# The last head of the second layer: V's split and Silu behind the first scores, its gates kept on chip, two output tiles loaded one head ahead

## The chip, the cores and the metric

The kernel runs on one core of one Trainium2 chip. The metric is the device time of one execution in microseconds. The engines are called as the profile calls them: PE (TensorE matmul), PEld (its weight load), DVE (VectorE), ACT (ScalarE), POOL (GpSimd) and SP (SyncE, which issues most DMAs).

## The reference

Two layers over 1024 latent tokens and 256 context tokens of width 1024. Layer 0 is multi-head latent attention, layer 1 differential attention; the change lies in layer 1, of which only the latent stream is returned.

```
q, k, v, gate = split(h @ w_in, 4)              # 8 heads of two 64-wide q/k pairs, v 128 wide; rope on q, k
for each head, m in (0, 1):                     # keys: 1024 latent and 256 context tokens
    o_m = softmax(q_m k_m^T / 8) v
o = rms_norm(o_1 - lam * o_2, g_sub) * (1 - lambda_init)
o = o * silu(gate)                              # all heads side by side: 1024 wide
x = layer_norm(alpha * x + ada_gate * (o @ out_w[1]), ln_g, ln_b)
```

## The kernel before

Values are split into a high and a low part, and a product is three matmuls (`mm3`: high x high, high x low, low x high). So nearly every operand has a pair of tiles: `vh`/`vl` for V, `ph`/`pl` for the turned probabilities, `oH`/`oL` for the output weight.

Layer 1 runs head by head (`H1` = 8), and in a head over eight query tiles of 128 rows. `step1` is one step. It issues for tile t the scores (`scores1`: PSUM banks `b`, maxima on DVE at L1360 and L1364, Exp on ACT at L1370, the combination of the two softmaxes on DVE at L1376), for tile t-2 the values (`values1`, L1391 to L1393, then `o` on ACT at L1396 and L1397), and for tile t-1 the turns of the probabilities (`turn1`, L1383) with their split into `ph` (ACT, L181) and `pl` (DVE, L182). Between these pieces it draws work from a generator `side`, by credits given in `SLOT1` or `SLOTO`. In heads 0 to 6 the side work is the projection of the next head (`prod_k1`, `prod_q1`, `prod_v1`) and the preparation of weights; the projection of V leaves V in `Vf`, the raw gates in `gg`, and a closure `top` in the list `later`, which splits V, applies the Silu and stores the gates in DRAM (`sg_d`, L1333). In head 6 the side work also holds the output weight: four slices by `out_w1`, four by `out_pre`, which loads and scales them into the buffers `z` and `res`.

In the last head (`last`, h = 7) the side work is the output projection. `out_open` runs ahead of its first step: it opens a pool for the gates (`g`, two buffers), loads the layer norm's gain, loads tiles 0 and 1 (`out_load`: the seven finished heads of `o` from `o_d`, all gates from `sg_d`, and their product on POOL at L1484) and splits the four prepared weight slices (L1473, L1474 and the helper `split` at L176 and L177). Each tile is then turned (`out_turns`, seven transposes at L1496), multiplied by the output weight (`out_tile1`, `mm3` at L185 to L187), given the eighth turn of the last head's slice, and normalised. In step t of the last head the side work is `out_tile1(t - 2)` with `out_turns(t - 1)` woven in; in step 2 `out_turns(0)` goes first; steps 0 and 1 have none.

The order on PE is the order in the program (`manual_schedule` with `MAN1 = 'P'`). On the other engines and on SP's queue a planner sets the order when the kernel is built, by program order among what its own cost model holds ready. Each engine then works its list in order. PSUM has eight banks, all under the tag `b` in this layer; a bank is bound to its next tile by the planner. Tiles of SBUF rotate by tag: `ws` has three buffers, `wsq` one, `p0` two, `p1` one, `vh` and `vl` two.

Of the kernel before, what the change touches and what calls it, by code (L numbers as in the profile page):

```python
# [9 lines left out]
F32 = mybir.dt.float32  # L10
# [3 lines left out]
AF = mybir.ActivationFunctionType  # L14
ALU = mybir.AluOpType
AX = mybir.AxisListType

P = 128
# [35 lines left out]
def hybrid_kernel(  # L54
# [40 lines left out]
    def spool(name, **kw):  # L95
        return tc.tile_pool(name=name, bufs=1, reuse_waits="tile", **kw)
# [5 lines left out]
    def rot(pool_, shape, dt, tag, bufs=1, first=False):  # L102

        if not first and (id(pool_), tag) in pre:
            return pre.pop((id(pool_), tag))
        t = pool_.tile(shape, dt, tag=tag, bufs=bufs, name=nm(tag))
        if first:
            pre[id(pool_), tag] = t
        return t
# [69 lines left out]
    def split16(hi, lo, src, scale):  # L179

        act.activation(hi, src, AF.Copy, scale=scale)  # L181
        dve.scalar_tensor_tensor(lo, src, scale, hi, op0=ALU.mult, op1=ALU.subtract)  # L182
# [384 lines left out]
    def chain(*gs):  # L567
        for g in gs:
            yield from g
# [406 lines left out]
    def w1(tag):  # L976
        sh, d, b = TAG1[tag]
        return rot(place[tag], sh, d, tag, b)
# [70 lines left out]
    with ow_ctx, spool("o0") as op0:  # L1049
# [96 lines left out]
        for t in range(8):  # L1146
# [53 lines left out]

    TAGP = {"cosB": ([P, SEQ], F32, 1), "sinB": ([P, SEQ], F32, 1), "rsw": ([P, 512], F32, 1),
            "kr": ([P, NTOK], F32, 1), "kH": ([P, NTOK], F16, 1), "kL": ([P, NTOK], F16, 1)}
    TAGV = {"rr": ([P, 512], F32, 1), "gg": ([P, SEQ // P, P], F32, 1), "Vf": ([P, NT, P], F32, 1)}

    TAGO = {"res": ([P, D], F32, 2), "z": ([P, D], F32, 2), "gb3": ([P, D], F32, 1),
            "bs": ([P, 2, 6], F32, 2), "mv": ([P, 4], F32, 2)}
# [9 lines left out]
    wo4 = a1.enter_context(spool("a1ow", side="right"))  # L1216
    oHL = [[wo4.tile([P, D], F32R, name=f"oH1{k}"), wo4.tile([P, D], F32R, name=f"oL1{k}")] for k in range(NOW)]
    gate1 = wo4.tile([P, D], F32, name="gate1")
    wv1 = prv.enter_context(spool("a1projv", side="right"))
    for k_, v_ in TAGV.items():  # L1220
        rot(wv1, v_[0], v_[1], k_, v_[2], first=True)
# [7 lines left out]
    def weave(main, side, at):  # L1229

        for i, v in enumerate(main):
            if i in at:
                next(side, None)
            yield v
        yield from side
# [67 lines left out]
    def prod_v1(h):  # L1303
        w, uv = wt[1], un[1]
        gg, Vf = w1("gg"), w1("Vf")
        vt[h] = vh, vl = w1("vh"), w1("vl")
        vT = w1("rr")[:, :CTX]
        ps = bank("b")
        for k in range(KT):
            mm3(ps[:, :CTX], w[k][0][:, :P], w[k][1][:, :P], h1H[:, k, SEQ:], h1L[:, k, SEQ:], k == 0, k == KT - 1)  # L1310
            if k % 2:
                yield 6 * CTX
        act.copy(vT, ps[:, :CTX])  # L1313
        for t in (0, 1, 2, 8, 3, 4, 9, 5, 6, 7):
            ts = slice(t * P, (t + 1) * P)
            ps = bank("b")
            if t < 8:
                for k in range(KT):
                    mm3(ps[:, :256], h1H[:, k, ts], h1L[:, k, ts], *w[k], k == 0, k == KT - 1)
                    if k % 2:  # L1320
                        yield 6 * 276
            else:
                pe.transpose(ps[:, :P], vT[:, (t - 8) * P:(t - 7) * P], idn)
                yield 256
            act.copy(Vf[:, t, :], ps[:, :P])
            if t < 8:
                act.copy(gg[:, t, :], ps[:, P:256])

        def top():
            split16(vh, vl, Vf, kc1)  # L1330
            g = gg.rearrange("p t d -> p (t d)")
            act.activation(g, g, AF.Silu, scale=uv)
            sp.dma_start(sg_d[1][:SEQ, h * P:(h + 1) * P].rearrange("(t p) d -> p t d", p=P), gg)  # L1333

        later.append(top)
        yield 0

    def scores1(h, t):
# [48 lines left out]
    def values1(h, t, ph, pl, sm):  # L1387
        vh, vl = vt[h]
        ps = bank("b")[:, :P]
        for kc in range(NT):  # L1390
            pe.matmul(ps, ph[:, kc, :], vh[:, kc, :], start=kc == 0, stop=False)  # L1391
            pe.matmul(ps, ph[:, kc, :], vl[:, kc, :], start=False, stop=False)  # L1392
            pe.matmul(ps, pl[:, kc, :], vh[:, kc, :], start=False, stop=kc == NT - 1)  # L1393
        o, o2, ss = w1("o1"), w1("o2"), w1("ss")
        pool.tensor_tensor(sm[:, 5:6], sm[:, 2:3], us1[h], op=ALU.mult)  # L1395
        act.activation(o, ps, AF.Copy, scale=sm[:, 5:6])  # L1396
        act.activation(o2, o, AF.Square, accum_out=ss[:, 0:1])  # L1397
        rstd_of(ss[:, 1:2], ss[:, 0:1], 1.0 / P, 1)
        if h == H1 - 1:
            oo, g = og[t]  # L1400
            c = slice(h * P, (h + 1) * P)
            dve.scalar_tensor_tensor(oo[:, c], o, ss[:, 1:2], g[:, c], op0=ALU.mult, op1=ALU.mult)
            return
        pool.tensor_scalar(o, o, ss[:, 1:2], None, op0=ALU.mult)
        sp.dma_start(o_d[1][t * P:(t + 1) * P, h * P:(h + 1) * P], o)
# [41 lines left out]
    def out_pre(k):  # L1447

        w = w1(("z", "res")[k % 2])
        sp.dma_start(w, out_w[1, k * P:(k + 1) * P, :])  # L1450
        yield
        if k % 2:
            act.activation(w, w, AF.Copy, scale=gsub)
        pool.tensor_tensor(w, w, gate1, op=ALU.mult)
        pre.append(w)
        yield

    def out_open():

        prv.close()  # L1460
        wg1 = a1.enter_context(spool("a1outg"))
        place["g"] = wg1
        TAG1["g"] = ([P, D], F32, 2)
        og["gb2"] = w1("wsq")
        bcast_row(og["gb2"], ln_g[1:2, :])
        rest = [big.tile([P, 5, D], F32R, tag=tg, name=nm("o1")) for tg in ("bigA", "bigB")]
        oHL.extend([r[:, k - NOW, :] for r in rest] for k in range(NOW, KT))
        out_load(0)
        for k, w in enumerate(pre):
            if k % 2:  # L1470
                split(*oHL[NOW + k], w, e_lo=pool)
            else:
                act.activation(oHL[NOW + k][0], w, AF.Copy, scale=gsub)  # L1473
                dve.scalar_tensor_tensor(oHL[NOW + k][1], w, gsub, fv(oHL[NOW + k][0]), op0=ALU.mult, op1=ALU.subtract)  # L1474
            if k == 0:
                out_load(1)

    def out_load(t):

        ts = slice(t * P, (t + 1) * P)  # L1480
        o, g = og[t] = w1("ws"), w1("g")
        sp.dma_start(o[:, :DH], o_d[1][ts, :DH])
        sp.dma_start(g, sg_d[1][ts, :])
        pool.tensor_tensor(o[:, :DH], o[:, :DH], g[:, :DH], op=ALU.mult)  # L1484

    oT = {}

    def out_turn(t, k0, n):

        o, _ = og[t]  # L1490
        if k0 == 0:
            oT[t] = [w1(tg).bitcast(F32R).rearrange("p (a b) -> p a b", a=KT) for tg in ("wx", "wy")]
        tH, tL = oT[t]
        tb = bank("b")
        for j in range(n):
            pe.transpose(tb[:, j * P:(j + 1) * P], o[:, (k0 + j) * P:(k0 + j + 1) * P], idn)  # L1496
        f = lambda x: x[:, k0:k0 + n, :].rearrange("p a b -> p (a b)")
        split(f(tH), f(tL), tb[:, :n * P])

    def out_turns(t):  # L1500
        if t >= SEQ // P:
            return
        out_turn(t, 0, 4)
        yield 1024
        out_turn(t, 4, 3)
        yield 768
# [57 lines left out]
    with tc.manual_schedule(engines={ENG[c] for c in MAN1}):  # L1564
# [38 lines left out]
        def v_last(h):  # L1603
            while later:
                later.pop(0)()
            out_early()
            yield from weave(prod_v1(h), chain(*[out_w1(k, lambda: w1("ws")) for k in range(NOW)],
                                               *[out_pre(k) for k in range(NOW, KT)]), range(1, 36, 2))

        g1 = gate_row1()  # L1610
        part = lambda h: (v for _, v in zip(range(4 if h else 0), g1))
        for h in range(H1):
            last = h == H1 - 1
            if not last:
                G = chain(weave(weave(chain(prod_k1(h + 1), prod_q1(h + 1, 0), prod_q1(h + 1, 1)), part(h), (1, 9, 17, 25)),
                                prod_w(h + 1, 1), WAT[0]),
                          weave(prod_v1(h + 1), prod_w(h + 2, 0), WAT[1]) if h + 2 < H1 else v_last(h + 1))
            else:
                while later:
                    later.pop(0)()  # L1620
                out_open()
            for t in range(SEQ // P):
                if last:
                    if t >= 2:
                        out_load(t)
                    G = weave(out_tile1(t - 2), out_turns(t - 1), (9, 12)) if t >= 2 else iter(())
                    if t == 2:
                        G = chain(out_turns(0), G)
                    credit[0] = 0
                step1((h, t), G, SLOT1 if not last else SLOTO)  # L1630
                if last:
                    for _ in G:
                        pass
            for _ in G:
                pass
        for t in range(SEQ // P - 2, SEQ // P):
# [79 lines left out]
```

## Time and profile before

| | |
|---|---|
| Time, median of 3 runs | 1776.72 us (1774.41 to 1779.07) |
| The profiled execution | 1777.68 us |
| its span, first to last instruction | 1775.8 us |
| PE busy | 1662.7 us, 94% |
| DVE busy | 1225.1 us, 69% |
| ACT busy | 1117.2 us, 63% |
| POOL busy | 822.2 us, 46% |
| mean granted clock of PE | 0.993 |

Times in the profile count from the first instruction. The last head runs from about 1615 us to the end. In a timeline a row gives start, length, engine, line, operation, the tile written and the tiles read, and in brackets how long the engine stood idle before it and what released it. A line of a helper (L176, L177, L181, L182, L185 to L187) serves many callers; the names of the tiles tell which.

### The profile page before, as it was taken

Reading aid. Unit: us, or ns where it says so; the run is one execution under the profiler, and the core shown is the slowest. Engines: PE = TensorE matmul, PEld = TensorE weight load, DVE = VectorE, ACT = ScalarE, POOL = GpSimd, SP = SyncE. Lnnn points to the kernel's source line nnn. Section 1 sums busy time; section 2 is a strip of 40 time slices with the busy share of each in tenths; the row PEclk is TensorE's granted clock in tenths of the full one; section 3 lists DMA queues with packets and bytes.
Section 4 is the critical chain, followed back from the end, with each engine's and each line's share of the span. In section 5 each row is a group of like instructions: output and inputs, shape, how many; then the busy total and the mean of one; then the engine's idle time right before and its main releaser. Section 6 shows DMA issues by size and latency. Waiting matters only on the chain. (4 is left out here: it accounts for less than half of the span.)

```text
span 1775.8 us, 36794 instructions
## 1 busy us (share of the span) xinstructions
PE 1662.7 (94%) x14564; PEld 1232.4 (69%) x14564; DVE 1225.1 (69%) x2037; ACT 1117.2 (63%) x2235; POOL 822.2 (46%) x740
## 2 busy tenths in 40 slices
PE   7999999999999999899999999999999999988998
PEld 7999966556666565577867666767676757666876
DVE  7658675566665667646855778787877777878664
ACT  2551177677777777845635676767677766758542
POOL 1432147667777676846552323231414132455454
PEclk9999999999999999999999999999999999999999
DMA  8258520110111112155532213131312122241332
GB/s 302 85 151 258 165 69 22 41 45 21 42 46 28 37 55 69 57 176 187 166 101 61 78 54 80 55 81 55 79 43 69 41 57 62 66 127 67 109 111 71
DMA packets 111225, 154.84 MB, mean 87 GB/s; under 512 B 13415, under 2 KB 84679, under 8 KB 111054
## 3 DMA queue, kind: packets, MB, share of 16 engines
q1 hardware_dynamic: 102654, 144.90, 27.5%
q10 hardware_dynamic: 8400, 7.61, 1.3%
q8 instruction: 114, 1.87, 0.4%
q14 instruction: 57, 0.47, 0.1%
HBM read 98.65 MB, written 27.07 MB: 71 GB/s over the span
## 5 line engine op out<-in xcount | busy, mean ns | idle before, releaser
L779 POOL TENSOR_TENSOR pl<-p,ph 128x1024 f16<-128x1024 f32 (+1 forms) x176 | 365.4, 2082 | 150.0 <-ACT ph L778 123.4
L1370 ACT ACTIVATE p<-ps_b,mx 128x512 f32<-128x512 f32 (+1 forms) x384 | 230.2, 616 | 65.6 <-DVE mx L1366 64.6
L777 ACT ACTIVATE p<-ps_a,esc 128x1024 f32<-128x1024 f32 (+1 forms) x176 | 189.0, 1074 | 97.4 <-PE ps_a L835 91.3
L759 DVE TENSOR_REDUCE mx<-ps_a 128x1 f32<-128x1024 f32 x128 | 155.2, 1222 | 131.2 <-PE ps_a L757 131.1
L778 ACT CAST ph<-p 128x1024 f16<-128x1024 f32 (+1 forms) x176 | 177.1, 1006 | 5.5
L1364 DVE TENSOR_REDUCE mx<-ps_b 128x1 f32<-128x512 f32 x256 | 165.4, 680 | 0.4 <-PE ps_b L1348 0.3
L848 PE MATMUL ps_d<-Vh,pl 128*128 128x65 f16 x1344 | 146.6, 194 | 3.1 <-POOL pl L779 3.1
L845 PE MATMUL ps_d<-Vh,ph 128*128 128x65 f16 x1344 | 148.7, 195 | 0.0
L847 PE MATMUL ps_d<-Vl,ph 128*128 128x64 f16 x1344 | 147.5, 193 | 0.0
L845 PEld LDWEIGHTS <-ph 128*128 128x128 f16 x1344 | 123.7, 98 | 18.3 <-issue 5.2
L1347 PE MATMUL ps_b<-KS,QS 128*128 128x512 f16 (+1 forms) x384 | 126.5, 347 | 7.7 <-DVE pl L182 4.5
L847 PEld LDWEIGHTS <-ph 128*128 128x128 f16 x1344 | 124.3, 99 | 12.3 <-issue 0.5
L1395 POOL TENSOR_TENSOR sm<-sm,us 128x1 f32<-128x1 f32 x64 | 18.5, 288 | 245.9 <-DVE sm L1374 241.9
L833 PE MATMUL ps_a<-qH,KH 100*128 100x512 f16 x320 | 122.6, 383 | 9.1 <-ACT p L777 4.3
L1348 PE MATMUL ps_b<-KS,Q 128*128 128x512 f16 (+1 forms) x384 | 129.7, 347 | 0.0
L1383 PE MATMUL ps_b<-idr,p 128*128 128x128 f32 x640 | 102.7, 276 | 28.3 <-ACT rr L1313 7.8
L182 DVE SCALAR_TENSOR_TENSOR pl<-ps_b,lcf,ph 128x512 f16<-128x512 f32 (+1 forms) x192 | 116.8, 653 | 14.3 <-ACT ph L181 14.3
L848 PEld LDWEIGHTS <-pl 128*128 128x128 f16 x1344 | 123.5, 98 | 4.3 <-POOL pl L779 4.2
L181 ACT ACTIVATE ph<-ps_b,lcf 128x512 f16<-128x512 f32 (+1 forms) x192 | 115.4, 649 | 13.2 <-PE ps_b L1383 13.2
L834 PE MATMUL ps_a<-qH,KL 96*128 96x512 f16 x320 | 122.5, 383 | 0.0
L835 PE MATMUL ps_a<-qL,KH 96*128 96x512 f16 x320 | 121.9, 381 | 0.0
L1383 PEld LDWEIGHTS ps_b<-idr,p 128*128 128x128 f32 x640 | 77.0, 141 | 54.2 <-ACT p L1370 10.9
(438 smaller groups left out, 5293.6 us busy)
## 6 DMA issues: line engine op xcount, KB each, us to landing
ws<-in_dw SPq DMA_DIRECT2D x28, 512.0 KB, 4.1
adw<-in_ada_w SPq DMA_DIRECT2D x24, 512.0 KB, 4.7
adaw<-in_ada_w SPq DMA_DIRECT2D x16, 512.0 KB, 7.9
g<-sg_d SPq DMA_DIRECT2D x16, 512.0 KB, 9.1
sg_d<-gg ACTq DMA_DIRECT2D x40, 128.0 KB, 3.6
o_d<-op SPq DMA_DIRECT2D x7, 640.0 KB, 3.8
xt<-in_xT SPq DMA_DIRECT2D x16, 256.0 KB, 4.4
wgs<-in_w_in SPq DMA_DIRECT2D x32, 128.0 KB, 3.2
```

Source lines behind the costliest of these rows:

```text
L759: dve.tensor_reduce(mx[:, t, 0:1], ps, axis=AX.X, op=ALU.max)
L777: act.activation(p32[:, :n], st, AF.Exp, scale=esc0)
L778: act.copy(ph[:, :n], p32[:, :n])
L779: pool.tensor_tensor(pl[:, :n], p32[:, :n], ph[:, :n], op=ALU.subtract)
L845: pe.matmul(pv[:, t, :], ph[:, ts], Vh[:, k, h, :], start=(k == kcs[0] and t == 0), stop=False, skip_group_check=True)
L847: pe.matmul(pv[:, t, :V0], ph[:, ts], Vl[:, k, h, :], start=False, stop=False, skip_group_check=True)
L848: pe.matmul(pv[:, t, :], pl[:, ts], Vh[:, k, h, :], start=False, stop=(k == NT - 1), skip_group_check=True)
L1347: pe.matmul(out, qs[m][:, ts], ks[m][:, c0:c0 + n], start=True, stop=False)
L1348: pe.matmul(out, q1[m][:, ts], ks[m][:, c0:c0 + n], start=False, stop=True)
L1364: dve.tensor_reduce(mx[:, 2 + 2 * m + i:3 + 2 * m + i], b, axis=AX.X, op=ALU.max, negate=True)
L1370: act.activation(p[m][:, c0:c0 + n], b, AF.Exp, bias=nb, accum_out=sm[:, 2 + 3 * m + i:3 + 3 * m + i])
L1383: pe.transpose(st[:, j * P:(j + 1) * P], pc[:, (k0 + j) * P:(k0 + j + 1) * P], idn)
```

## The change

`prod_v1` of the last head no longer puts `top` in `later`: it leaves `Vf`, `gg` and the gates' scale in the dictionary `og`. A new function `out_gates` runs behind step 1 of the last head. It takes a new pair `vh`/`vl`, splits V, closes the pool of `Vf`, opens a pool in its place with one tile `g7`, and writes the Silu of the gates there. The last head's gates are not stored to DRAM; L1402, which applies them to the last head's slice, reads `g7`.

`gg` moves to a pool that stays open. Tiles 2 to 7 load their seven eighths of the gates into it, so the pool `a1outg` with two buffers `g` goes. Tiles 0 and 1 are loaded in head 6, by `out_first` in the chain of `v_last`, with their gates in `wsq`: tile 0 between `out_w1` and `out_pre`, tile 1 behind `out_pre`. The gain `gb2`, which also lives in `wsq`, comes behind them.

The split of the four weight slices moves from `out_open` to the generator `out_split`, the side work of step 0, and `out_turns(0)` becomes the side work of step 1.

```
     def prod_v1(h):
...
-        later.append(top)
+        if h < H1 - 1:
+            later.append(top)
+        else:
+            og.update(Vf=Vf, gg=gg, uv=uv)
...
         if h == H1 - 1:
-            oo, g = og[t]
-            c = slice(h * P, (h + 1) * P)
-            dve.scalar_tensor_tensor(oo[:, c], o, ss[:, 1:2], g[:, c], op0=ALU.mult, op1=ALU.mult)
+            dve.scalar_tensor_tensor(og[t][:, DH:], o, ss[:, 1:2], og["g7"][:, t, :], op0=ALU.mult, op1=ALU.mult)
             return
...
     def out_open():
-        prv.close()
-        wg1 = a1.enter_context(spool("a1outg"))
-        place["g"] = wg1
-        TAG1["g"] = ([P, D], F32, 2)
         og["gb2"] = w1("wsq")
...
-        out_load(0)
+    def out_split():
         for k, w in enumerate(pre):
...
-            if k == 0:
-                out_load(1)
+            yield 0
+
+    def out_gates():
+        vt[H1 - 1] = vh, vl = w1("vh"), w1("vl")
+        split16(vh, vl, og["Vf"], kc1)
+        prv.close()
+        wg1 = a1.enter_context(spool("a1outg", side="right"))
+        og["g7"] = wg1.tile(GG[0], GG[1], name="g7")
+        flat = lambda x: x.rearrange("p t d -> p (t d)")
+        act.activation(flat(og["g7"]), flat(og["gg"]), AF.Silu, scale=og["uv"])
 
-    def out_load(t):
+    def out_load(t, g_tag="gg"):
         ts = slice(t * P, (t + 1) * P)
-        o, g = og[t] = w1("ws"), w1("g")
+        o, g = w1("ws"), w1(g_tag)
+        og[t] = o
         sp.dma_start(o[:, :DH], o_d[1][ts, :DH])
-        sp.dma_start(g, sg_d[1][ts, :])
+        if g_tag == "gg":
+            g = g.rearrange("p t d -> p (t d)")
+        sp.dma_start(g[:, :DH], sg_d[1][ts, :DH])
         pool.tensor_tensor(o[:, :DH], o[:, :DH], g[:, :DH], op=ALU.mult)
...
         def v_last(h):
...
             yield from weave(prod_v1(h), chain(*[out_w1(k, lambda: w1("ws")) for k in range(NOW)],
-                                               *[out_pre(k) for k in range(NOW, KT)]), range(1, 36, 2))
+                                               out_first(0), *[out_pre(k) for k in range(NOW, KT)],
+                                               out_first(1)), range(1, 36, 2))
+
+        def out_first(t):
+            out_load(t, "wsq")
+            yield
...
             else:
-                while later:
-                    later.pop(0)()
                 out_open()
             for t in range(SEQ // P):
                 if last:
                     if t >= 2:
                         out_load(t)
-                    G = weave(out_tile1(t - 2), out_turns(t - 1), (9, 12)) if t >= 2 else iter(())
-                    if t == 2:
-                        G = chain(out_turns(0), G)
+                    G = (out_split(), out_turns(0))[t] if t < 2 else weave(out_tile1(t - 2), out_turns(t - 1), (9, 12))
                     credit[0] = 0
                 step1((h, t), G, SLOT1 if not last else SLOTO)
                 if last:
                     for _ in G:
                         pass
+                    if t == 1:
+                        out_gates()
```

More of the change, by code (lines that the diff above doesn't have):

```diff
@@ L1202, in hybrid_kernel @@
             "kr": ([P, NTOK], F32, 1), "kH": ([P, NTOK], F16, 1), "kL": ([P, NTOK], F16, 1)}
-    TAGV = {"rr": ([P, 512], F32, 1), "gg": ([P, SEQ // P, P], F32, 1), "Vf": ([P, NT, P], F32, 1)}
+    TAGV = {"rr": ([P, 512], F32, 1), "Vf": ([P, NT, P], F32, 1)}
+    GG = [P, SEQ // P, P], F32, 1
     TAGO = {"res": ([P, D], F32, 2), "z": ([P, D], F32, 2), "gb3": ([P, D], F32, 1),
@@ L1218, in hybrid_kernel @@
     gate1 = wo4.tile([P, D], F32, name="gate1")
+    rot(wo4, GG[0], GG[1], "gg", GG[2], first=True)
+    place["gg"], TAG1["gg"] = wo4, GG
     wv1 = prv.enter_context(spool("a1projv", side="right"))
@@ L1305, in prod_v1 @@
         gg, Vf = w1("gg"), w1("Vf")
-        vt[h] = vh, vl = w1("vh"), w1("vl")
+        vh, vl = w1("vh"), w1("vl")
+        vt[h] = vh, vl
         vT = w1("rr")[:, :CTX]
@@ L1488, in out_turn @@
     def out_turn(t, k0, n):
-        o, _ = og[t]
+        o = og[t]
         if k0 == 0:
```

## The prediction

> **What bounds the kernel now.** I read the page first, then the stretches around the edited place, then the waits of TensorE there, then the four engines' timelines between 1614 and 1642 us. From the page:
>
> ```profile
> span 1775.8 us, 36794 instructions
> ```
>
> The windows view gives per row: the stretch, its length, busy us (and count) of PE, PEld, DVE, ACT and POOL, the granted clock, the DMA share and GB/s.
>
> ```profile
> 1626.00:1632.00 6.00, 6.00 (x34) 3.28 (x32) 4.55 (x12) 4.85 (x17) 4.35 (x3) 0.54 0.77 305
> ...
> 1650.00:1656.00 6.00, 6.00 (x33) 4.50 (x33) 3.57 (x7) 1.71 (x4) 0.47 (x1) 1.00 0.27 76
> ```
> ```profile
> 1640.00:1740.00 100.00, 99.09 (x619) 78.47 (x617) 66.94 (x134) 50.91 (x133) 49.16 (x50) 1.00 0.34 109
> ```
>
> From 1640 us on TensorE is the bound: 99.09 us busy of 100 at full clock, and the program ends a fixed tail behind its last matmul. The change moves no matmul out of or into that phase except seven transposes. So the end moves with the moment at which the phase starts, and the question is what TensorE loses before it. The waits view, for TensorE between 1614 and 1665 us, has one large entry (us in total, times, longest):
>
> ```profile
> PE ps_b L1383 <- DVE pl L182: 5.8, 1, 5.8
> ```
>
> TensorE's timeline (start, length, instruction, and in brackets the idle time before it and who ended it):
>
> ```profile
> 1614.82 0.27 PE L1347 MATMUL ps_b<-KS,QS 128*128 128x256 f16 x1
> ...
> 1616.98 0.22 PE L1391 MATMUL ps_b<-vh,ph 128*128 128x128 f16 x1
> ...
> 1618.66 1.04 PE L1383 MATMUL ps_b<-idr,p 128*128 128x128 f32 x8
> 1625.53 0.69 PE L1383 MATMUL ps_b<-idr,p 128*128 128x128 f32 x2 [5.83 <-DVE pl L182]
> 1626.18 0.37 PE L1347 MATMUL ps_b<-KS,QS 128*128 128x256 f16 x1
> ...
> 1630.40 0.31 PE L1391 MATMUL ps_b<-vh,ph 128*128 128x128 f16 x1
> ...
> 1634.55 1.28 PE L1383 MATMUL ps_b<-idr,p 128*128 128x128 f32 x10 [1.78 <-DVE p L1376]
> 1635.67 0.27 PE L1347 MATMUL ps_b<-KS,QS 128*128 128x256 f16 x1
> ...
> 1639.51 0.93 PE L1496 MATMUL ps_b<-idr,ws 128*128 128x128 f32 x7
> 1641.08 0.50 PE L185 MATMUL ps_b<-oH,wx 128*128 128x512 f32 x1 [0.64 <-ACT wx L176]
> ```
>
> Read it as steps of the last head, one per query tile: scores (L1347/L1348), values of two tiles ago (L1391 to L1393), turns of one tile ago (L1383). At full clock a set of scores takes 1616.98 - 1614.82 = 2.16 us, values 1618.66 - 1616.98 = 1.68, turns 1635.67 - 1634.55 = 1.12, the seven turns of an output tile 0.93. Three steps and the seven turns are 3 x (2.16 + 1.68 + 1.12) + 0.93 = 15.81 us of work. They occupy 1614.82 to 1641.08, which is 26.26 us: 10.45 us are lost. That is the most the change can win there. The loss has two parts: the idle 5.83 us, and behind it a slow clock (0.54 granted between 1626 and 1632, so about 5.5 us at half speed; the scores take 1630.40 - 1626.18 = 4.22 us).
>
> Why TensorE stood still shows in ScalarE's order, and in the two others':
>
> ```profile
> 1615.14 1.17 ACT L1473 ACTIVATE o<-z,gsub 128x1024 fp32r<-128x1024 f32 x1
> ...
> 1616.50 1.40 ACT L181 ACTIVATE vh<-Vf,kc 128x1280 f16<-128x1280 f32 x1
> 1617.91 1.28 ACT L1332 ACT_TABLE_LOAD   x1
> 1619.21 1.15 ACT L1332 ACTIVATE gg<-gg,uw 128x1024 f32<-128x1024 f32 x1
> 1620.26 1.03 ACT L176 CAST o<-res 128x1024 fp32r<-128x1024 f32 x1
> ...
> 1623.18 1.25 ACT L181 ACTIVATE ph<-ps_b,lcf 128x512 f16<-128x512 f32 x2
> 1624.45 1.28 ACT L1370 ACT_TABLE_LOAD   x1
> 1625.75 0.69 ACT L1370 ACTIVATE p<-ps_b,mx 128x512 f32<-128x512 f32 x1
> ...
> 1631.62 0.69 ACT L1370 ACTIVATE p<-ps_b,mx 128x512 f32<-128x512 f32 x1 [1.05 <-DVE mx L1366]
> ...
> 1633.40 0.37 ACT L1396 ACTIVATE o<-ps_b,sm 128x128 f32<-128x128 f32 x1
> 1634.43 0.69 ACT L1370 ACTIVATE p<-ps_b,mx 128x512 f32<-128x512 f32 x1 [0.66 <-DVE p L1376]
> ...
> 1635.21 1.71 ACT L181 ACTIVATE ph<-ps_b,lcf 128x512 f16<-128x512 f32 x3
> ...
> 1639.76 0.37 ACT L1396 ACTIVATE o<-ps_b,sm 128x128 f32<-128x128 f32 x1 [1.43 <-POOL ss L160]
> ...
> 1640.46 0.94 ACT L176 CAST wx<-ps_b 128x512 fp32r<-128x512 f32 x2
> ```
> ```profile
> 1619.01 1.54 DVE L182 SCALAR_TENSOR_TENSOR vl<-Vf,kc,vh 128x1280 f16<-128x1280 f32 x1
> ...
> 1631.74 1.06 DVE L1375 SCALAR_TENSOR_TENSOR sm<-sm,nlam 128x1 f32<-128x1 f32 x1
> ...
> 1635.93 1.80 DVE L182 SCALAR_TENSOR_TENSOR pl<-ps_b,lcf,ph 128x512 f16<-128x512 f32 x3 [1.53 <-ACT ph L181]
> ...
> 1639.57 0.21 DVE L1375 SCALAR_TENSOR_TENSOR sm<-sm,nlam 128x1 f32<-128x1 f32 x1
> ```
> ```profile
> 1628.66 4.12 POOL L1484 TENSOR_TENSOR ws<-ws,g 128x896 f32<-128x896 f32 x2 [1.65 <-DMA g<-sg_d]
> ```
>
> ScalarE does V's split, a table load, the Silu, four casts of the output weight, and only at 1623.18 the split `ph` that TensorE's next PSUM bank waits for; then a second table load, and the first Exp of the head at 1625.75.
>
> **Part by part, V's split and Silu.** Ahead of the first Exp the change takes away 1.40 + 1.28 + 1.15 + 1.28 = 5.11 us of ScalarE and 1.54 of VectorE. The idle 5.83 then shrinks to under a microsecond, and the slow clock behind it goes too. But this is not the gain, because ScalarE is full to about 1638 and becomes what is late next. The same split now stands behind step 1 in the program, it needs the old buffer of `vh` (so the values of the head before must be done), and the values of step 2 need it. Nothing but scores is queued ahead of those values on TensorE, and the whole output tile 0 is queued behind them. So the phase starts when V's split is done. ScalarE's work up to there, from 1615.14: one cast and two copies 1.36 (to 1616.50), three casts 2.92 (1620.26 to 1623.18), two tiles of Exp, each two groups of 1633.40 - 1631.62 = 1.78, so 7.12; two `o` pairs at 1640.46 - 1639.76 = 0.70, so 1.40; two `ph` splits at 1.71, so 3.42; the two casts of the first turns, 0.94; V's split 1.40. Sum 18.56, so 1633.70. Its waits on VectorE in this stretch (1.05 and 0.66) stay: 1635.4. VectorE's half takes 1.54: 1636.95. Then the values, 1.68, and output tile 0 starts at 1638.63, where today it starts at 1641.08. That is the late end of my bounds: a gain of 2.45 us.
>
> The early end: if V's split slips into a hole of ScalarE, the values of step 2 wait for their own chain only. The Exps of step 0 begin at about 1615.14 + 1.36 + 2.92 + 1.25 = 1620.67 in place of 1625.75, 5.08 earlier. From there on the chain is the present one, without the delay that I read in the row of 1.06 us, a 128x1 operation beside GpSimd's multiply of 4.12; without one beside it the same line takes 0.21, so 0.8 less. The values, today at 1639.51 - 1.68 = 1637.83, come 5.9 earlier, at 1631.9; the seven turns no longer stand behind them (0.93) and the waits of 0.64 at the phase's start go: a gain of 7.5 us. I take 4.0, nearer to the late end, since the split is last in program order of all that competes with it and ScalarE has only the two short holes quoted, none of 1.40.
>
> The Silu with its two loads, 1.28 + 1.15 + 1.28 = 3.71, now lies beside output tile 0. There ScalarE is busy 1.71 of 6 us (the row of 1650), so the cover is 4.3 us in each 6; I cost it at nothing. If that cover fails the cost is 3.71. Its reader is the turn of the last head's slice, late in tile 0. [...]
>
> **Gates on chip.** The store of the last head's gates and an eighth of each gate load go; SP and the DMA queues are not the bound, so nothing. The buffer that gates are loaded into is now single and free only behind the Silu.
>
> ```profile
> g<-sg_d SPq DMA_DIRECT2D x16, 512.0 KB, 9.1
> ```
> ```profile
> 1649.66 0.44 PE ps_b L1496 x4
> ...
> 1666.60 0.44 PE ps_b L1496 x4
> ```
>
> A load of 9.1 us and a multiply of 4.12 / 2 = 2.06 make 11.2, and in the chain of waits the same transposes come 16.94 us apart, so one buffer turns round in time: 0, and up to a few us per tile only if a load took over 14.
>
> **Tiles 0 and 1 loaded one head ahead.** Two loads of gates and two multiplies (4.12 us of GpSimd) leave 1628 to 1633 and go into the end of head 6, past the four loads of output weights on SP's queue and the four multiplies `out_pre` on GpSimd's.
>
> ```profile
> 1586.56 2.36 POOL L1454 TENSOR_TENSOR z<-z,gate 128x1024 f32<-128x1024 f32 x1 [4.99 <-DMA z<-in_out_w]
> ```
> ```profile
> 1587.88 1.15 ACT L1453 ACTIVATE res<-res,gsub 128x1024 f32<-128x1024 f32 x1 [3.82 <-DMA res<-in_out_w]
> ```
>
> GpSimd's hole of 4.99 holds both multiplies. But ScalarE already stands 3.82 us for such a load, and what is queued behind it there is Exp and `ph`. Each gate load ahead of it may add its transfer; from 9.1 us for a landing alone to nothing when it overlaps. I take 0, by the present wait, which TensorE rides out; the bounds are a gain of 1 us (shorter GpSimd queue later) and a cost of 10.
>
> The seven turns of tile 0 between the values and turns of step 1 fill a wait there: their 0.93 is in the sum above.
>
> **Sum.** The profiled execution took 1777.68 us, its span of 1775.8 and 1.88 around it. 1777.68 - 4.0 = 1773.7. The median of the runs before is 1776.72, 0.96 lower, so I forecast 1772.7. About 0.3%, 5.3 us, is what a measurement can tell from no change.
>
> **Rivals.** (B) V's split slips in early, gain 7.5: 1769.2. For it: step 1's Exps share one buffer `p1`, the wait of 0.66 on L1376, so ScalarE is not always served. Against: no hole of 1.40 today. The most there is to win is the lost 10.45: 1766.3.
>
> (C) TensorE stands for V's split long enough for the clock to drop. Today 5.83 us of idling were followed by half clock; this one was not (full speed behind it):
>
> ```profile
> 1001.17 0.55 PE L1383 MATMUL ps_b<-idr,p 128*128 128x128 f32 x3 [2.35 <-ACT rr L1313]
> ```
>
> So the point from which it decides lies between 2.35 and 5.83 us. The third scores end today at 1637.83, where the values follow; 5.08 earlier, with the Exps that free their banks, is 1632.75, and the wait to 1636.95 is 4.2. The price: 5.5 us at half clock lose 2.75, so the gain of the late end, 2.45, is gone: 1777.0. If the Exps of step 2 also get ahead of the split (two groups, 3.56), it ends at 1780.6, and with a table switch between them higher. [...]
>
> (D) Slower: the early gate loads push the output weights back, ScalarE and GpSimd stand in order for them in head 6, and TensorE runs dry there. One landing, 9.1 us, beyond today's 3.82 decides; TensorE's cover is what its eight banks hold. Price at the bound: 10 us less the gain of 4.0, so 1782.7. Against: today's wait costs TensorE little.
>
> (E) It does not do what it says: if ScalarE's queue puts the split back ahead of the Exps as it becomes ready, nothing is won. It can't: the values of the head before must be done first, and they come after the first scores. No chance.
>
> **How the numbers follow.** A, 2.45 to 6.5 gained, 0.44, of which the part above 5.3 is 0.14; B 0.24; C 0.18, of which 0.08 lies over 5.3 slower; D 0.14. Faster by over 0.3%: 0.14 + 0.24 = 0.38. Within: 0.30 + 0.10 = 0.40. Slower: 0.08 + 0.14 = 0.22. Both signs hold much of it. A's own range is 1770.2 to 1774.3. The range for 8 in 10 runs from 1767.3, which leaves out the top of B, to 1781.6, which leaves out the worst of C and half of D.
>
> **What would show it.** Right: no idle of 5.8 us on TensorE near 1620, granted clock 1.00 there; `vh` of the last head on ScalarE near 1634 to 1636 and the values of step 2 released by `vl` L182; the first L185 of output tile 0 some 3 to 4 us earlier than 1641; 99% busy behind it as now. Wrong: a row of TensorE waiting 3 us or more on `vl`, with a slow clock behind it (C); `vh` near 1630 (B); longer waits of L1453 and L1454 on their loads and more TensorE idling between 1570 and 1614 (D).

## The result and the profile after

The changed kernel takes 1785.97 us (median of 6 runs, 1783.68 to 1788.88), the kernel before beside it 1774.58 (1773.57 to 1779.07). The ratio is 1.0061 with a 95% interval of 1.0049 to 1.0073: slower by 0.6%, some 11 us. The forecast was 1772.7 with a range of 1767.3 to 1781.6, so the prediction was wrong, in sign and in range. The profiled execution after took 1783.68 us. From its page:

```profile
span 1781.7 us, 36792 instructions
```

The two traces issue the same matmuls in the same order, but for the seven turns of tile 0, so each matmul's start can be compared with its counterpart's. The last small idle before the disturbed stretch is the same instruction in both, here TensorE's timeline of before and then of after:

```profile
1577.08 0.63 PE L1383 MATMUL ps_b<-idr,p 128*128 128x128 f32 x4 [1.42 <-DVE p L1376]
```
```profile
1571.47 0.63 PE L1390 MATMUL ps_b<-idr,p 128*128 128x128 f32 x4 [1.41 <-DVE p L1383]
...
1592.77 1.12 PE L1390 MATMUL ps_b<-idr,p 128*128 128x128 f32 x4 [9.19 <-ACT p L1377]
...
1618.72 0.27 PE L1354 MATMUL ps_b<-KS,QS 128*128 128x256 f16 x1
...
1625.87 0.44 PE L1390 MATMUL ps_b<-idr,p 128*128 128x128 f32 x2 [2.27 <-ACT p L1377]
...
1629.01 0.58 PE L1354 MATMUL ps_b<-KS,QS 128*128 128x512 f16 x1 [1.87 <-DVE pl L182]
...
1632.37 0.31 PE L1398 MATMUL ps_b<-vh,ph 128*128 128x128 f16 x1
...
1647.26 0.63 PE L185 MATMUL ps_b<-oH,wx 128*128 128x512 f32 x1
```

There this execution was 5.6 us ahead, gathered in parts that the change doesn't touch. At the first scores of the last head it is 3.9 behind (1618.72 against 1614.82). So head 6 lost 9.5 us, nearly all of it in a wait of 9.19, where the same matmul of before waited 0.56. The stage that the change was aimed at, from the first scores to the first matmul of output tile 0, takes 1647.26 - 1618.72 = 28.54 us where it took 26.26. Behind it the phase that TensorE bounds is as long as before, 125.4 us to the last matmul against 125.9. The three parts, 9.5 + 2.3 - 0.4, make 11.4, the difference between the medians.

**Head 6.** The first output-weight load on SP's queue in before, and then the timelines of SP's queue, GpSimd and ScalarE after:

```profile
1580.96 0.43 SPq L1450 DMA_DIRECT2D z<-in_out_w  x1
```
```profile
1566.44 1.53 SPq L1495 DMA_DIRECT2D ws<-o_d  x2
1573.30 0.32 SPq L1498 DMA_DIRECT2D wsq<-sg_d  x1
...
1579.58 0.51 SPq L966 DMA_DIRECT2D wsq<-in_ln_g  x1
1581.22 0.33 SPq L1410 DMA_DIRECT2D o_d<-o  x1
...
1582.07 0.46 SPq L1455 DMA_DIRECT2D z<-in_out_w  x1
```
```profile
1570.05 3.22 POOL L1499 TENSOR_TENSOR ws<-ws,wsq 128x896 f32<-128x896 f32 x1 [3.11 <-DMA ws<-o_d]
...
1577.47 2.08 POOL L1499 TENSOR_TENSOR ws<-ws,wsq 128x896 f32<-128x896 f32 x1 [4.05 <-DMA wsq<-sg_d]
...
1580.58 0.61 POOL L1409 TENSOR_SCALAR o<-o,ss 128x128 f32<-128x128 f32 x1
...
1589.66 2.34 POOL L1459 TENSOR_TENSOR z<-z,gate 128x1024 f32<-128x1024 f32 x1 [8.31 <-DMA z<-in_out_w]
```
```profile
1590.90 1.15 ACT L1458 ACTIVATE res<-res,gsub 128x1024 f32<-128x1024 f32 x1 [12.45 <-DMA res<-in_out_w]
```

SP's queue stands from about 1568 to 1573.30 at the load of tile 1's gates. `wsq` has one buffer, and tile 0's multiply frees it only at 1573.27. Then the store of o waits for its own scaling, which stands behind tile 1's multiply on GpSimd (1580.58). The output-weight loads stand behind both, and the first goes out at 1582.07. In before it went at 1580.96, which is 1580.96 - 5.6 = 1575.4 in this trace's time, so it is 6.7 late. ScalarE then stands 12.45 us in order for the weight, with the Exps behind it that TensorE waits for. Of the 8.63 by which this wait grew (3.82 in before), the later issue of ScalarE's own load (1582.63 against 1581.48 - 5.61) is 6.8, and 1.9 is a slower way from issue to use: 8.27 us against 6.40. What slowed it was not separated; the layer norm's gain, which lives in `wsq` too, now goes out 2.5 us ahead of the weights (1579.58), where in before it went at 1507.25. The two loads from `o_d` are not new there: before has them ahead of the weights as well (1572.05 and 1573.26).

**The last head.** ScalarE and VectorE after:

```profile
1623.11 1.36 ACT L181 ACTIVATE vh<-Vf,kc 128x1280 f16<-128x1280 f32 x1
1625.04 0.69 ACT L1377 ACTIVATE p<-ps_b,mx 128x512 f32<-128x512 f32 x1 [0.57 <-DVE mx L1373]
...
1630.97 1.28 ACT L1488 ACT_TABLE_LOAD   x1
1632.27 1.15 ACT L1488 ACTIVATE g<-gg,uw 128x1024 f32<-128x1024 f32 x1
...
1636.99 1.28 ACT L1377 ACT_TABLE_LOAD   x1
1638.28 0.69 ACT L1377 ACTIVATE p<-ps_b,mx 128x512 f32<-128x512 f32 x1
```
```profile
1626.13 2.25 DVE L182 SCALAR_TENSOR_TENSOR vl<-Vf,kc,vh 128x1280 f16<-128x1280 f32 x1
```

V's split still stands ahead of the first Exp. The Silu with both table loads has only moved from ahead of step 0's Exps to ahead of step 1's. The first Exp comes 6.32 us after the first scores (10.93 before, 5.85 in my sum), but step 1's first comes 19.56 after them, where it came 1631.62 - 1614.82 = 16.80 after in before: what step 0 won is gone there, and 2.8 more. Behind the first of two short idles (2.27 and 1.87, above) the clock was also slow:

```profile
1626.00:1632.00 6.00, 3.90 (x14) 1.56 (x15) 5.11 (x8) 5.39 (x14) 1.03 (x1) 0.59 0.38 123
```

### The profile page after: what moved, and what is told of

Read it like the earlier page. It is cut to its first block, busy times and chain, and to the rows that moved or that the text cites. A ratio compares the mean times of both kernels' runs of the same rounds, so it can differ in the third digit from the quotient of the medians.

```text
span 1781.7 us, 36792 instructions
## 1 busy us (share of the span) xinstructions
PE 1662.0 (93%) x14564; PEld 1234.0 (69%) x14564; DVE 1223.6 (69%) x2037; ACT 1117.2 (63%) x2235; POOL 818.0 (46%) x740
## 3 DMA queue, kind: packets, MB, share of 16 engines
q8 instruction: 114, 1.87, 0.4%
## 5 line engine op out<-in xcount | busy, mean ns | idle before, releaser
L1402 POOL TENSOR_TENSOR sm<-sm,us 128x1 f32<-128x1 f32 x64 | 17.1, 268 | 249.6 <-DVE sm L1381 239.9
```

## The experiments

Each kernel was timed in five rounds beside the kernel before, whose medians were 1776.05 to 1776.37 (1774.58 beside the change). Runs of one kernel lie 2 to 9 us apart, so a difference of 3 us between two kernels is known to within 1 to 2 (95% interval of the means). The last columns are from one trace each. "Head 6" is what the kernel lost against before between about 1520 us and the first scores of the last head, by the same matmuls; "stage" is the time from the first scores of the last head to the first matmul of output tile 0.

| kernel | median us | ratio to before, 95% interval | head 6 | stage |
|---|---|---|---|---|
| before | 1776.2 | | 0 | 26.3 |
| the change | 1785.97 | 1.0061 [1.0049, 1.0073] | +9.5 | 28.5 |
| c_held | 1780.18 | 1.0015 [1.0004, 1.0026] | +2.2 | 29.6 |
| d_silu | 1777.31 | 0.9997 [0.9987, 1.0007] | +2.4 | 25.9 |
| e_vlate | 1774.27 | 0.9981 [0.9973, 0.9990] | +2.6 | 23.1 |
| b_ahead | 1784.36 | 1.0036 [1.0023, 1.0049] | +9.8 | 25.2 |
| f1_mul1 | 1773.02 | 0.9979 [0.9970, 0.9988] | +2.5 | 21.3 |
| **f2_mul01** | **1770.00** | **0.9962 [0.9949, 0.9974]** | -0.4 | 23.5 |
| g_vonly | 1777.32 | 1.0008 [0.9999, 1.0016] | +2.5 | 26.3 |
| h_split | 1775.84 | 1.0002 [0.9993, 1.0012] | +0.6 | 25.9 |
| k_lasthead | 1780.70 | 1.0029 [1.0020, 1.0039] | +8.9 | 21.3 |
| i_nosilu | 1770.96 | 0.9969 [0.9958, 0.9981] | -1.1 | 23.0 |
| j_low | 1773.76 | 0.9989 [0.9980, 0.9998] | +0.3 | 23.9 |

`issue_behind(x)` is an edge of order alone: the instruction comes behind x in its engine's list, with no wait added.

**c_held: tile 1's loads behind the output-weight loads.**

```
-            out_load(t, "wsq")
+            with issue_behind(og.get("preld")):   # the last load of out_pre
+                out_load(t, "wsq")
```

> The changed kernel with one difference: tile 1's two loads of head 6 are issued on SP's queue behind the last output-weight load, so that no load stands in the queue for GpSimd's multiply of tile 0. The bytes are the same. T1 (in-order wait): in the changed kernel SP stood about 5.3 us at the load of tile 1's gates (1573.30, behind the multiply that starts at 1570.05 and has one buffer to free), the output-weight loads came 5 to 7 us late and TensorE lost 9.5 us in head 6. Without that wait the loss in head 6 goes: TensorE's wait of 9.2 us at L1390 falls under 1 us and the time falls by 7 to 9.5, to 1776.5 to 1779. T1' (traffic): the extra transfers themselves delay the output weights; the loss stays at 5 us or more, time 1783 or more.

The same bytes, 5.8 us less: 1780.18. Against the kernel before in the same rounds it loses 3.8, where the change lost 11.4. ScalarE's wait for the weight is 4.32 us in place of 12.45, TensorE's 1.06 in place of 9.19. So the standstill of SP's queue made the greater part of head 6's loss (T1); 2.2 us stayed, and the time lies 1 us above T1's bounds. The gain's load, which waits for tile 1's multiply, moves behind the weights with it (1591.52).

```profile
1583.56 1.15 ACT L1463 ACTIVATE res<-res,gsub 128x1024 f32<-128x1024 f32 x1 [4.32 <-DMA res<-in_out_w]
```

**b_ahead: the loads ahead alone, put into the kernel before.**

```
-                                               *[out_pre(k) for k in range(NOW, KT)]), range(1, 36, 2))
+                                               out_first(0), *[out_pre(k) for k in range(NOW, KT)],
+                                               out_first(1)), range(1, 36, 2))
...
```

Not shown are `out_first` itself, which loads and multiplies as in the change, and the last eighth of these gates, which is loaded in the last head.

> The kernel before with one part of the change: the seven eighths of the loads of tiles 0 and 1 and their multiplies stand in head 6 where the change puts them, with the gates in the single buffer wsq. Only the last head's eighth of their gates is loaded in the last head. T1 (in-order wait on the single buffer): TensorE's loss in head 6 appears here too, 7 to 9.5 us, while the last head may win 0 to 2 from the shorter queue of GpSimd: 1780 to 1784. T4 (the loss needs the rest of the change, such as the other places of the buffers): 1773 to 1777.

1784.36, 0.4 above T1's upper end: the loss appears with before's last head too, with the same stand of SP's queue (from about 1574 to 1579.31). T4 falls.

```profile
1572.44 1.53 SPq L1616 DMA_DIRECT2D ws<-o_d  x2
1579.31 0.32 SPq L1617 DMA_DIRECT2D wsq<-sg_d  x1
```
```profile
1597.10 1.15 ACT L1453 ACTIVATE res<-res,gsub 128x1024 f32<-128x1024 f32 x1 [12.63 <-DMA res<-in_out_w]
```

**f1_mul1 and f2_mul01: the multiplies behind the output weight's.** Both start from e_vlate (below). f1 issues tile 1's multiply behind the last `out_pre` multiply on GpSimd (`prem`), f2 tile 0's as well. f2's edit:

```
         sp.dma_start(g[:, :DH], sg_d[1][ts, :DH])
-        pool.tensor_tensor(o[:, :DH], o[:, :DH], g[:, :DH], op=ALU.mult)
+        if g_tag == "wsq" and t == 0:
+            og["mul0"] = o, g
+            return
+        with issue_behind(og["prem"] if g_tag == "wsq" else None):
+            pool.tensor_tensor(o[:, :DH], o[:, :DH], g[:, :DH], op=ALU.mult)
...
         def out_first(t):
...
+            if t == 1:
+                o, g = og["mul0"]
+                with issue_behind(og["prem"]):
+                    pool.tensor_tensor(o[:, :DH], o[:, :DH], g[:, :DH], op=ALU.mult)
```

> The kernel with tile 1's loads held, the Silu late and V's split late (1774.3 us, 2.1 under before), and besides GpSimd's multiply of tile 1 is issued behind its last output-weight multiply. In that kernel's trace VectorE's combination L1383 took 3.35 us beside this multiply where it takes 1.55 elsewhere, and TensorE lost 2.0 us in head 6 against before, 0.7 of it ahead of that place. T5 (the two engines slow each other when the multiply meets the combination): 1 to 1.6 us faster, L1383 back at 1.55. T5' (the multiply meets the next combination instead, or the stretch has another cause): within 0.5 of it.

> The same with tile 0's multiply also behind the last output-weight multiply, so that GpSimd's work in head 6 up to there is in the order of before. T6 (the rest of head 6's loss, 0.7 us, comes from tile 0's multiply: it holds GpSimd's scaling of o, the store of o waits for that on SP's queue, and the output-weight loads stand behind the store): the output weight's wait on ScalarE falls from 4.5 to the 3.8 us of before, head 6 loses under 0.5 us, and the time is 1.5 to 2 under the kernel with V's split late, 1772 to 1773. T6' (the transfers of the extra loads delay the output weights): 0.7 stays and the time equals that with tile 1's multiply moved alone.

In e_vlate VectorE and GpSimd met, and the combination took 3.35 us (by the table's matmuls its head 6 lost 2.6, more than the 2.0 that I had put down):

```profile
1589.51 3.35 DVE L1383 SCALAR_TENSOR_TENSOR p<-p,sm,p 128x1280 f32<-128x1280 f32 x1
```
```profile
1589.42 2.10 POOL L1506 TENSOR_TENSOR ws<-ws,wsq 128x896 f32<-128x896 f32 x1
```

f1 brings it back to 1.55, but its trace lost as much in head 6, at a lower clock. VectorE's timeline and the windows of f1:

```profile
1593.88 1.55 DVE L1383 SCALAR_TENSOR_TENSOR p<-p,sm,p 128x1280 f32<-128x1280 f32 x1
```
```profile
1590.00:1595.00 5.00, 4.20 (x25) 3.08 (x25) 2.19 (x4) 5.00 (x17) 3.98 (x3) 0.73 0.61 241
```
h_split has the same head 6, was not slowed there (granted 1.00 from 1590 to 1595 us), and loses 0.6. The times of f1 and e_vlate can't be told apart, so T5 is left open in time. f2 loses nothing in head 6; its weight wait is below before's 3.82:

```profile
1583.45 1.15 ACT L1463 ACTIVATE res<-res,gsub 128x1024 f32<-128x1024 f32 x1 [3.28 <-DMA res<-in_out_w]
```

1770.00 is 3.0 under f1 in the same rounds and 4.3 under e_vlate, more than T6 expected. T6' is not borne out: from its issue to its use ScalarE's first weight takes 6.03 us in f2, 6.54 in e_vlate and 6.40 in before, so beside the extra transfers it was at most half a microsecond slower. It is not quite excluded, since tile 1's gate load waits for tile 0's multiply and so moved with it (1596.03 in f2, 1579.21 in e_vlate). This version beats both kernels.

**d_silu: from c_held, the Silu behind step 1's Exps.**

```
+        with issue_behind(og["exp"]):             # the last Exp of step 1
             act.activation(flat(og["g7"]), flat(og["gg"]), AF.Silu, scale=og["uv"])
```

> The kernel with tile 1's loads held, and besides the Silu of the last head is issued on ScalarE's queue behind the last Exp of step 1, where the changed kernel has it between the Exps of step 0 and step 1. T2 (ScalarE's 1.28 + 1.15 + 1.28 = 3.71 us of Silu and table loads ahead of step 1's Exps is what ate the last head's gain): output tile 0 starts 3 to 4 us earlier after the last head's first scores than 26.2 us, and the time is 3 to 4 under the kernel with the loads held alone. T2' (the order of ScalarE's work does not matter, its sum does): 0 to 1 us under it.

2.9 us faster, and the stage goes from 29.6 to 25.9: T2, except that I had it start 3 to 4 under 26.2.

**e_vlate: from d_silu, V's split behind step 0's Exps.**

```
+        with issue_behind(og["exp0"]):            # the last Exp of step 0
             split16(vh, vl, og["Vf"], kc1)
```

> The kernel with tile 1's loads held and the Silu behind step 1's Exps, and besides V's split is issued on ScalarE's queue behind the last Exp of step 0, where the changed kernel has it ahead of the first (1623.11, 1.36 us). T3 (the split ahead of the Exps still delays them: ScalarE 1.36 and VectorE 2.25 us ahead of the second softmax of step 0): 1 to 2 us under the kernel with the late Silu alone, the waits of TensorE at 1625.9 and 1629 (2.27 and 1.87) shrink and the slow clock behind them goes. T3' (V's split is then late for the values of step 2): TensorE waits 1 to 4 us on the low part of V there, and the time is 0 to 3 over it.

3.0 us faster (T3 had 1 to 2). ScalarE's order in this trace is the one of my early end, with V's split ahead of step 1's Exps and the Silu behind them, and TensorE hardly waits for V. Of T3's signs one failed: a wait of 2.53 for the first Exps stays, and a slow clock behind it: the scores from 1620.36 to 1624.18 took 3.82 us, where a set at full clock took 2.16 in before.

```profile
1619.53 0.69 ACT L1377 ACTIVATE p<-ps_b,mx 128x512 f32<-128x512 f32 x1 [1.12 <-DVE mx L1373]
...
1624.01 1.40 ACT L181 ACTIVATE vh<-Vf,kc 128x1280 f16<-128x1280 f32 x1
...
1628.37 0.69 ACT L1377 ACTIVATE p<-ps_b,mx 128x512 f32<-128x512 f32 x1 [0.55 <-DVE p L1383]
...
1633.60 1.28 ACT L1495 ACT_TABLE_LOAD   x1
```
```profile
1612.18 0.27 PE L1354 MATMUL ps_b<-KS,QS 128*128 128x256 f16 x1
...
1620.36 0.37 PE L1354 MATMUL ps_b<-KS,QS 128*128 128x256 f16 x1 [2.53 <-ACT p L1377]
...
1634.42 0.23 PE L1400 MATMUL ps_b<-vh,pl 128*128 128x128 f16 x1 [0.42 <-DVE pl L182]
...
1635.30 0.48 PE L185 MATMUL ps_b<-oH,wx 128*128 128x512 f32 x1
```

**g_vonly: from c_held, V's split late, nothing said of the Silu.**

> The kernel with tile 1's loads held (1780.2), and V's split alone issued on ScalarE behind the last Exp of step 0; nothing is said of the Silu. The planner's order, as built, then has Silu and table loads behind step 1's Exps by itself, one piece of the turned probabilities later than it. T7 (the place of V's split decides alone; the Silu follows it): within 1 us of the kernel with both held, 1774.3. T7' (the Silu ahead of that last piece costs 1.28 + 1.15 of the 3.7): 1.5 to 3 over it.

1777.32: 3.1 us above e_vlate (T7'). The Silu goes behind step 1's Exps by itself, yet ahead of one piece of `ph`, and TensorE's values stand for that piece:

```profile
1636.59 0.23 PE L1398 MATMUL ps_b<-vh,ph 128*128 128x128 f16 x1 [2.21 <-ACT ph L181]
```

**k_lasthead: the change with the last head of e_vlate and its own head 6.** Its edits are the two of d_silu and e_vlate, without the held loads.

> The changed kernel (1786.0) with its head 6 as it is, and in the last head V's split behind step 0's Exps and the Silu behind step 1's. T9 (two faults that add up): head 6 keeps its loss of about 9.5 us against before, the last head gains about 3.7 in place of losing 1.85, so 5.5 to 6 us under the changed kernel: 1779.5 to 1781. T9' (the stall of head 6 swallows or changes the last head's part): 1783 or more.

1780.70, as T9 has it: head 6 still loses 8.9, the stage takes 21.3. The two faults add up.

**i_nosilu: from f2_mul01, no Silu.**

```
-        act.activation(flat(og["g7"]), flat(og["gg"]), AF.Silu, scale=og["uv"])
+        act.activation(flat(og["g7"]), flat(og["gg"]), AF.Copy, scale=1.0)
```

> The kernel with both multiplies of head 6 moved and the last head in the late order (1770.0), with the Silu of the last head left out: ScalarE copies the raw gates to g7 in its place, so there are no two table loads (2.56 us of ScalarE) and the last head's gates are wrong. T10 (the Silu and its loads lie beside output tile 0, as I predicted at no cost): within 1 us of it. T10' (the cover fails): 2 to 3 us faster.

1770.96, no faster: behind step 1's `ph` the two table loads lie beside other work (T10). This kernel leaves the Silu out, so its gates are raw; a copy of 1.10 us stands in the place of the Silu's 1.15, so only the loads are priced.

**h_split and j_low: the output weight's splits later.** VectorE's two lows are the low halves of two weight slices. h, from f1_mul1, issues ScalarE's two L1481 and these lows a step later; j, from f2_mul01, holds only the lows behind step 0's maxima:

```
...
+                            with issue_behind(og["mx"]):   # the last maximum of step 0
                                 dve.scalar_tensor_tensor(oHL[NOW + k][1], w_, gsub, fv(oHL[NOW + k][0]), op0=ALU.mult, op1=ALU.subtract)
```

> The kernel with tile 1's multiply moved, and besides the splits of the four prepared weight slices leave step 0 for step 1: ScalarE's two scalings L1481 (1.17 each) and VectorE's two lows (2.20 each) come behind the Exps of step 1, the two casts stay. T8 (ScalarE's and VectorE's load ahead of the first Exps is what TensorE's remaining waits of 2.5 and 1.7 us in the last head come from): 1 to 3 us faster than without this. T8' (the same work then stands ahead of output tile 0 and its Exps): 0 to 3 slower, with a wait of TensorE near the first L185.

> The kernel with both multiplies of head 6 moved and the last head in the late order (1770.0), with VectorE's two lows of the output-weight slices (1.28 and 2.18 us) issued behind the maxima of step 0 instead of between them. T11 (the wait of 2.5 us that TensorE still has in the last head, for an Exp that waits for those maxima, and the slow clock behind it go): 1.5 to 3 us faster. T11' (the lows then stand ahead of the split pl and of step 1's maxima, which are as urgent): 0 to 2 us slower, with a wait of TensorE on pl.

Both lost: h about 2.8 us against f1, j 3.8 against f2 (T11' had 0 to 2). The first Exp of the last head does come sooner, 5.1 us after the first scores in both, but the waits move, to the values in h and to `pl` in j (T8', T11'):

```profile
1634.70 0.27 PE L1398 MATMUL ps_b<-vh,ph 128*128 128x128 f16 x1 [3.51 <-DVE sm L1382]
```
```profile
1622.20 0.61 PE L1354 MATMUL ps_b<-KS,QS 128*128 128x512 f16 x1 [2.92 <-DVE pl L182]
```

## Why the prediction was wrong

**"Each gate load ahead of it ... I take 0."** This term is the largest error: 0 forecast, 9.5 us measured. Case D, at 0.14 and a price of 10, had the size and the place (ScalarE and GpSimd in order for late output weights, TensorE dry). It had the wrong cause, transfers pushed back by a gate's landing, so that its 10 lies near 9.5 is luck. What failed is that I moved the loads ahead of the weight loads on SP's queue without asking what each of them itself waits for. Tile 1's gate load waits for tile 0's multiply, since `wsq` is single, and the store of o waits for work that stands behind tile 1's multiply. c_held and b_ahead show that the queue's stand makes most of it. Of the wait that grew by 8.63, 6.8 are later issue; the 1.9 of slower landing may be traffic, which was not separated. "GpSimd's hole of 4.99 holds both multiplies" failed as well, since both run ahead of the hole or, in c_held to e_vlate, tile 1's behind it.

**"(E) ... It can't ... No chance."** E happened. I had V's split wait for "the old buffer of `vh`". But `vh` has two buffers, and the values of the head before read the other: `vh` is written at 1623.11 in the trace after, and step 1's values of head 6 (L1398 at 1632.37) come later. With no wait the split went ahead of the Exps once `Vf` was there. The place in the program did not hold it; e_vlate's edge of order did.

**"The Silu with its two loads ... now lies beside output tile 0 ... at nothing."** By its place in the change it lay ahead of step 1's Exps; d_silu minus c_held prices that at 2.9 us of time and 3.7 of the stage, and my price for a lost cover was 3.71. In its intended place its two loads cost nothing that was measured (i_nosilu), so this step was right of a kernel that was not the one changed.

**The sum, 4.0 us.** With V's split and the Silu in late places and head 6 undisturbed, f2_mul01, the gain is 6.05 us between the medians, and 0.26% to 0.51% or 4.6 to 9.1 by the ratio. The last head alone shows 3.7 in e_vlate's trace, and 3.3 to 5.5 over the four traces that have it in this form (e, f1, f2, k). So the size lies in A's range, but not by A's mechanism, and that is in part luck. A had output tile 0 start when V's split is done. In e_vlate the split slipped in early, 11.8 us after the first scores (1624.01 - 1612.18), as in B, VectorE's half was done at 1631.04, and step 2's values began at 1633.05. B's 7.5 was not reached either. The 5.08 that I carried along the chain is 3.6 at the first Exp (7.35 after the first scores, 10.93 before) and 0.6 at step 1's (16.19 against 16.80). The first Exp waits for maxima among which VectorE's two lows stand, rows that I had not counted (with the lows behind the maxima, in h_split and j_low, it comes at 5.1); step 1's waits for the combination (0.55). VectorE in e_vlate:

```profile
1614.72 1.27 DVE L1482 SCALAR_TENSOR_TENSOR o<-z,gsub,o 128x1024 fp32r<-128x1024 f32 x1
...
1617.11 2.19 DVE L1482 SCALAR_TENSOR_TENSOR o<-z,gsub,o 128x1024 fp32r<-128x1024 f32 x1
1619.23 0.26 DVE L1373 TENSOR_SCALAR mx<-mx 128x1 f32<-128x1 f32 x1
```

**C.** TensorE never stood for V's split at the values of step 2, where I priced it: with the split late, in e_vlate, these wait 0.42 for `pl`. In the trace after it stood at step 1's scores instead (1.87), for a `pl` that VectorE splits behind the `vl` of 2.25.

## What to carry to other kernels

When a load is moved ahead on an in-order queue, look up what the load itself waits for. Here the buffer was single, so the load waited for its last reader (tile 0's multiply, to 1573.27 in the trace after), and everything behind it on SP's queue waited too, 5.3 us (1567.97 to 1573.30). Putting it behind the urgent loads helped by 5.8 us (c_held); a second buffer was not tried. A later place in the program alone did not hold V's split back (it ran at 1623.11 in the trace after, ahead of the first Exp at 1625.04); the edge of order in e_vlate did (1624.01, the first Exp at 1619.53). Count the buffers of the tag before a wait is counted on.

## What the runs showed of the hardware

The clock was granted differently after the same idles. e_vlate's two idles in head 6 (0.94 and 1.41 us) left full clock, c_held's (0.95 and 1.41) did not. TensorE's timeline and the windows of c_held, then those of e_vlate:

```profile
1558.06 0.66 PE L1390 MATMUL ps_b<-idr,p 128*128 128x128 f32 x4 [0.95 <-DVE p L1383]
1560.78 1.12 PE L1390 MATMUL ps_b<-idr,p 128*128 128x128 f32 x4 [1.41 <-ACT o L1403]
```
```profile
1556.89:1560.31 3.42, 1.53 (x9) 0.68 (x7) 2.68 (x5) 0.56 (x1) 2.92 (x3) 1.00 0.07 19
...
1562.00:1566.00 4.00, 4.00 (x25) 2.56 (x24) 1.90 (x5) 4.00 (x14) 3.54 (x6) 0.79 0.32 76
```
```profile
1557.98 0.66 PE L1390 MATMUL ps_b<-idr,p 128*128 128x128 f32 x4 [0.94 <-DVE p L1383]
1560.69 0.66 PE L1390 MATMUL ps_b<-idr,p 128*128 128x128 f32 x4 [1.41 <-ACT o L1403]
```
```profile
1558.90:1562.32 3.42, 2.01 (x12) 0.97 (x10) 1.22 (x4) 2.62 (x8) 2.63 (x4) 1.00 0.18 46
...
1562.00:1566.00 4.00, 4.00 (x32) 2.99 (x31) 2.48 (x7) 4.00 (x14) 3.65 (x6) 1.00 0.33 79
```

In c_held both idles fell mostly into one stretch of 3.41 us, in which TensorE was busy 1.53, and the clock fell at its end. In e_vlate such a stretch ended between the two, and the two stretches were busy 2.46 and 2.01. These are the slow stretches of the traces before and after between 1400 and 1740 us, each behind the 3.41 us ahead of it, first before, then after:

```profile
1621.25:1624.67 3.42, 0.00 (x0) 0.00 (x0) 3.38 (x5) 3.40 (x6) 3.29 (x2) 1.00 0.55 156
1624.67:1631.49 6.82, 5.96 (x25) 3.19 (x26) 5.37 (x11) 5.79 (x17) 5.17 (x3) 0.50 0.80 308
```
```profile
1582.75:1586.16 3.41, 0.83 (x8) 0.49 (x6) 0.00 (x0) 0.00 (x0) 0.00 (x0) 1.00 0.75 179
1586.16:1596.40 10.24, 3.17 (x14) 2.38 (x15) 0.67 (x3) 5.50 (x17) 6.62 (x3) 0.50 0.61 245
...
1623.71:1627.12 3.41, 1.02 (x6) 0.65 (x7) 3.41 (x5) 2.84 (x7) 3.32 (x2) 1.00 0.52 156
1627.12:1633.95 6.83, 4.96 (x24) 2.71 (x23) 5.84 (x12) 5.93 (x13) 0.19 (x1) 0.50 0.27 79
...
1640.77:1644.19 3.42, 1.76 (x8) 0.32 (x5) 3.38 (x8) 3.02 (x11) 0.33 (x2) 1.00 0.45 134
1644.19:1647.60 3.41, 3.27 (x29) 3.27 (x30) 2.70 (x6) 0.01 (x1) 2.54 (x3) 0.50 0.00 0
```

They last 6.82, 10.24, 6.83 and 3.41 us, one to three times 3.41, and those of after begin 40.96 and 17.07 us apart, 12 and 5 times 3.413. In the 3.41 us ahead of them TensorE was busy 0.00, 0.83, 1.02 and 1.76. At 1627.12 the clock fell before the idle of 1.87 had begun (1629.01 - 1.87 = 1627.14). Steps of the same length, counted back from 1624.67 in before and from 1627.12 in after, hold stretches with as little work behind which the clock stayed full, two in before and one in after:

```profile
1454.00:1457.41 3.41, 1.48 (x9) 0.78 (x8) 3.23 (x6) 3.41 (x7) 0.19 (x1) 1.00 0.69 210
...
1474.48:1477.89 3.41, 1.57 (x15) 1.26 (x13) 3.41 (x6) 0.35 (x3) 2.51 (x3) 1.00 0.43 105
```
```profile
1449.63:1453.04 3.41, 1.64 (x8) 0.78 (x8) 3.41 (x7) 3.41 (x9) 0.15 (x1) 1.00 0.82 233
```

So there is no single length of an idle, "between 2.35 and 5.83 us", from which the clock drops, as I had it: little more than an idle of 2.27 was enough. The work in such a stretch gives no sharp point either, since the clock fell behind 1.53 (c_held) and 1.76 (after) and stayed full behind 1.48, 1.57 (before) and 1.64 (after). What decides between these was not shown.

VectorE and GpSimd held each other up where the combination met the multiply of an output tile. In e_vlate the combination took 3.35 us, where it takes 1.55 elsewhere, beside a multiply of 2.10 that began 0.09 earlier. In the trace after it was the multiply that took longer, 3.22 for 2.08, beside a combination of 1.54 that began 0.27 earlier (1569.78 against 1570.05). In both the one that began later was slowed. From the start of the first to the end of the second the pair of e_vlate took 1589.51 + 3.35 - 1589.42 = 3.44 us and that of after 1570.05 + 3.22 - 1569.78 = 3.49, where the two operations one after the other would be 2.10 + 1.55 = 3.65 and 1.54 + 2.08 = 3.62. So they ran almost in turn. Why was not shown.
